# Opening a decoder step with three output tiles instead of two

## The chip, the cores and the metric

The kernel runs on one core of one Trainium2 chip. The metric is device time in microseconds (us) of one execution. In the profile PE is the matrix engine, PEld its weight loads, DVE the vector engine, ACT the scalar engine, POOL the GpSimd engine and SP the engine that only issues transfers (DMAs).

## The reference, cut to what matters

One inference step of a two-layer decoder (one pooling layer, one sliding-window attention layer) for 1024 prompt tokens and 8 single decode tokens, width 2048, all in fp32. The part that concerns us is the first product of the first layer:

```python
def pool_layer(x, prefix, pos, w_in, w_grp, scale, w_out, g_ln, b_ln):
    z = x @ w_in                       # (1032 x 2048) @ (2048 x 4096)
    u, gate = z[..., :D_POOL], z[..., D_POOL:]
    d, new_state = multiscale_pool(u, prefix, pos)
    d = jnp.einsum('btgc,gce->btge', d.reshape(B, T, N_POOL_GROUPS, POOL_GROUP), w_grp)
    ...
    y = (d * jax.nn.silu(gate)) @ w_out
    return layer_norm(ALPHA * x + y, g_ln, b_ln), new_state
```

After it come a shared key/value projection, the attention layer with a second pair of projections, and two layer norms.

## The kernel before, in words

There are four large projections, which the code calls phases: `ai` and `ao` (in and out of the pooling layer), `bi` and `bo` (in and out of the attention layer). Each is a two-by-two block product with seven block products instead of eight (Winograd's form of Strassen's method), numbered by `idx` 0 to 6. The tokens form two parts (512 prompt tokens, and 512 prompt plus 8 decode tokens); depth and output channels form two halves each, in tiles of 128. A **unit** is one block product for one output tile: `pos` is the tile, `idx` the block product, `ph` the phase, and `u.t` is its start in **ticks**, the planner's clock; a unit of group A takes two ticks. Groups are worked in the order A (`idx` 0 and 5), C (1, 3, 6), B (2, 4). `idx` 0 of the phase `ai` reads the even depth tiles of the first token part; `idx` 5 reads the odd ones (the "odd inputs") and adds into the same PSUM bank.

Every fp32 operand is rounded to the fp32r format on ACT (the *high* part, a CAST) and the rest is taken on DVE (the *low* part, high subtracted from the original). A product is then three matmuls with 512 columns: high weight by high input, high by low, low by high. A unit of group A has eight depth blocks, so 24 matmuls.

PSUM gives these products a ring of three banks (`psD`), one bank per output tile. After `idx` 0 ACT copies the bank, negated, to SBUF, which POOL's queue stores to DRAM (`post`, then `nai`); `idx` 5 goes on adding in the same bank, and after it ACT copies the bank out as the result. The bank is then free for a later tile.

The order of the work is written by the program itself. PE, DVE and ACT run strictly in the order in which the Python code records instructions. `end()` closes a tick: it runs tasks fixed to a tick (`on`, e.g. loads 11 ticks ahead of a unit), then "soft" tasks (`soft`: not before one tick, due at another) as far as the engines look idle by rough cost figures. `rounds` queues the two rounding steps of a unit's weights that way; `x_cast`, `x_low` and `x_next` do the same for inputs, and `xhold` keeps the rounding of four odd inputs back until a tick. SBUF is 53 slots of 128 by 1040 fp32, handed out oldest-freed first, halves apart where half is enough.

The start is written out by hand. `start` warms PE with nine matmuls on zeros, then loads the weights of the first two tiles in pieces (a quarter, a quarter, a half of 512 KB) and the four even inputs in halves (260 KB each), all on SP's queue but one on ACT's, and splits each piece into high and low as it comes. The load of the first unit of `idx` 5 and the four odd inputs follow. `opening` then records the matmuls of the first two units: depth blocks 0 to 4 side by side (block 0 of tile 0, block 0 of tile 1, block 1 of tile 0, and so on), blocks 5 to 7 one tile after the other. Inside it, after each tile's last block, the odd inputs' roundings are recorded and the bank is copied. From then on `run_unit` does one unit after the other. Transfers from SP and ACT take turns on eight completion semaphores, and an issue waits for the transfer that last used its semaphore: at most eight are under way.

Of the kernel before, what the change touches and what calls it, by code (L numbers as in the profile page):

```python
# [72 lines left out]
L_LOAD, L_CAST, L_LOW = 11, 6, 4  # L73
# [87 lines left out]
class Kern:  # L161
# [169 lines left out]
    def plan(self):  # L331

        U = self.units = []
        for ph in PH:
            for grp, idxs in GROUPS:
                for pp in range(len(POS[ph]) // 2):
                    two = 2 * pp, 2 * pp + 1
                    U0 = lambda p, i, hs, **kw: U.append(Unit(kind="p", ph=ph, grp=grp, pos=p, idx=i, hs=hs, **kw))
                    if grp == "A":
                        for i in idxs:  # L340
                            if i == 0 and pp in DEEP.get(ph, ()):
                                U.append(Unit(kind="q", ph=ph, grp=grp, pos=two[0], idx=0, hs=(FULL, None) * 2))
                                continue
                            for p in two:
                                U0(p, i, (FULL, None))
                    elif (ph, grp) == ("bo", "B") and pp > 1:
                        continue
                    else:
                        for p in two:
                            for i in idxs:  # L350
                                U0(p, i, HV)
                    if ph == "ai" and pp % 4 == 3:
                        g = pp // 4
                        for c, gg in {"A": ((0, g),), "C": ((0, g + 2),), "B": ((1, g), (1, g + 2))}[grp]:
                            for h in range(2):
                                U.append(Unit(kind="g", ph=ph, grp=grp, c=c, g=gg, h=h, hs=HV))
        for h in HV:
            for p in (4, 6):
                for i in (2, 4):
                    for q in (p, p + 1):  # L360
                        U.append(Unit(kind="p", ph="bo", grp="B", pos=q, idx=i, hs=(h,), keep=h is HV[0]))
        t = 0
        self.first, self.tick, self.need, self.lastu = {}, {}, {}, {}
        for u in U:
            u.t = t
            t += len(u.hs)
# [24 lines left out]
    def rounds(self, t, e, early=L_CAST + 2):  # L391

        def cast():
            if "cast" not in e["did"]:
                e["did"].add("cast")
                if "raw" not in e and "load" in e:
                    e["load"]()
                e["hi"] = self.mem.full()
                self.nc.scalar.copy(e["hi"].r[:, :1024], e["raw"].a[:, :1024])  # L399

        def low():
            if "low" not in e["did"]:
                e["did"].add("low")
                cast()
                s = e.pop("raw")
                o = e["lo"] = self.mem.full()
                self.nc.vector.tensor_sub(o.r[:, :1024], s.a[:, :1024], e["hi"].a[:, :1024])  # L407
                s.free()

        e["did"] = set()  # L410
        e["cast"], e["low"] = cast, low
        def cast_task():
            cast()
            self.soft("v", self.i + 1, t - L_LOW, low)

        e["queue"] = lambda: self.soft("a", max(t - early, 3 * (t > 5)), t - L_CAST + 1, cast_task)
        if "load" in e:
            e["queue"]()

# [302 lines left out]
    def opening(self, *us):  # L722
        nc, cs = self.nc, FULL
        W = [self.w_get(u) for u in us]
        ps = [self.psD() for _ in us]
        for p, u in enumerate(us):
            self.bank[u.ph, u.pos, cs.start] = ps[p]
        todo = [(k, p) for k in range(5) for p in range(2)] + [(k, p) for p in range(2) for k in (5, 6, 7)]

        def three(k, p, zs):  # L730
            h, l = (a.rv(2, TMAX)[:, k % 2, cs] for a in self.x_get(("ai", 0, k // 2)))
            wh, wl = (a.r[:, k * P : (k + 1) * P] for a in W[p])
            for z in zs:
                a, b = ((wh, h), (wh, l), (wl, h))[z]
                nc.tensor.matmul(ps[p], a, b, start=k == 0 and z == 0, stop=k == 7 and z == 2, skip_group_check=True)

        for n, (k, p) in enumerate(todo):
            if n == 0:
                for p in (0, 1):
                    three(0, p, (0,))  # L740
                for p in (0, 1):
                    three(0, p, (1, 2))
            elif n > 1:
                three(k, p, range(3))
            if n == 12:
                self.w_done(us[0])
                self.x_cast(("ai", 5, 0))
                self.x_low(("ai", 5, 0))
                self.post(us[0], cs)
                self.x_cast(("ai", 5, 1))  # L750
                self.x_low(("ai", 5, 1))
            if n == 15:
                self.w_done(us[1])
                self.post(us[1], cs)
                for j in (2, 3):
                    self.x_cast(("ai", 5, j))
            if n % 4 == 3:
                self.end()

# [1432 lines left out]
    def start(self):  # L2192
# [6 lines left out]
        es = [u.ent for u in self.units[:4]]  # L2199
        ks = [self.xl.pop(0) for _ in range(4)]  # L2200
        W, X = ([self.mem.full() for _ in range(n)] for n in (2, 4))
        ws = [slice(256 * i, 256 * i + 256) for i in range(4)]
        xs = [slice(TMAX * i, TMAX * i + TMAX) for i in range(2)]
        src = [self.x_src(k)[1] for k in ks]
        w = [self.quads("ai", p)[0] for p in range(2)]

        def wload(p, c):
            nc.sync.dma_start(W[p].a[:, c], w[p][:, c])

        wload(0, ws[0])  # L2210
        nc.scalar.dma_start(X[0].a[:, xs[0]], src[0][:, 0, :])
        wload(1, ws[0])
        nc.sync.dma_start(X[0].a[:, xs[1]], src[0][:, 1, :])
        for p in range(2):
            wload(p, ws[1])
        for j in range(1, 4):
            for i in range(2):
                nc.sync.dma_start(X[j].a[:, xs[i]], src[j][:, i, :])
            if j == 1:
                for p in range(2):  # L2220
                    wload(p, slice(512, 1024))
        es[2]["load"]()
        for n in range(4):
            self.x_load(self.xl[0])
        es[3]["load"]()
        for j in range(4):
            self.xhold["ai", 5, j] = 3
        nc.sync.dma_start(self.cst[:], io["cst"])
        nc.sync.dma_start(self.prm[:], io["prm"])
        nc.sync.dma_start(self.mki[:], io["mki"])  # L2230
        wn, xn = ([(self.mem.full(), self.mem.full()) for _ in range(n)] for n in (2, 4))

        def split(s, n, c, late=False):
            nc.scalar.copy(n[0].r[:, c], s.a[:, c])
            low = lambda: nc.vector.tensor_sub(n[1].r[:, c], s.a[:, c], n[0].a[:, c])
            return low if late else low()
# [1 line left out]
        low = split(W[0], wn[0], ws[0], True)  # L2238
        split(X[0], xn[0], xs[0])
        low()  # L2240
        split(W[1], wn[1], ws[0])
        split(X[0], xn[0], xs[1])
        for p in range(2):
            split(W[p], wn[p], ws[1])
        for i in range(2):
            split(X[1], xn[1], xs[i])
        for p in range(2):
# [35 lines left out]
    def run(self):  # L2283
# [35 lines left out]
        for g in range(2):  # L2319
            t = f["ai", "B"] + 40 * g  # L2320
# [166 lines left out]
```

## Time and profile before

| | |
|---|---|
| median of 3 runs | 2275.99 us (2271.91 to 2276.68) |
| profiled execution | 2273.81 us |
| its span, first to last instruction | 2272.0 us |
| mean granted PE clock | 0.999 |
| PE busy | 2262.4 us, 17312 matmuls |
| DVE busy | 1598.4 us |
| ACT busy | 1136.1 us |
| memory traffic | 239 GB/s over the span |

The time of a run is some 2 us longer than the span of the profiled execution. Matmuls are pipelined, and the profile gives a matmul's duration from its issue to its modelled end, so "busy" on PE also covers waits that are shorter than a matmul. The pace of PE is therefore read from the start times of its matmuls.

### The profile page before, as it was taken

What the parts mean: (1) busy time and instruction counts of PE and PEld (TensorE: products, weight loads), DVE (VectorE), ACT (ScalarE), POOL (GpSimd) and SP (SyncE); (2) the same over time, 40 slices, a digit from 0 to 9 for tenths busy, and PEclk for the clock granted to TensorE, in tenths of its full rate; (3) what the DMA queues carried; (4) which work ended last, traced back from release to release, by engine and by line L of the source; (5) the groups of instructions that cost most, each with busy time, mean ns of one, the idle gap of its engine ahead of it and who ended that gap; (6) DMA issues with size and microseconds to landing.
All of it is one profiled execution on the core that took longest, in us unless ns stands there. A gap on an engine that the chain in (4) does not pass through costs nothing.

```text
span 2272.0 us, 42903 instructions
## 1 busy us (share of the span) xinstructions
PE 2262.4 (100%) x17312; PEld 2130.5 (94%) x17312; DVE 1598.4 (70%) x2009; ACT 1136.1 (50%) x2372; POOL 197.8 (9%) x418
## 2 busy tenths in 40 slices
PE   9999999999999999999999999999999999999998
PEld 7889999999999899999888899999999998889998
DVE  7667746746667587685786876666566879687688
ACT  6344333343334443454576644545647678553365
POOL 0101001100100111000011010101000000111000
PEclk9999999999999999999999999999999999999999
DMA  9859757673657898888488776666754556898873
GB/s 305 314 209 350 233 213 256 227 249 117 243 184 261 276 336 291 292 304 297 153 295 301 245 244 205 230 195 220 244 169 124 177 189 224 284 356 304 301 250 132
DMA packets 190262, 556.43 MB, mean 245 GB/s; under 512 B 26096, under 2 KB 31600, under 8 KB 190064
## 3 DMA queue, kind: packets, MB, share of 16 engines
q1 hardware_dynamic: 147936, 401.82, 54.0%
q0 software_dynamic: 41984, 151.61, 17.4%
q8 instruction: 135, 2.21, 0.4%
q14 instruction: 63, 0.52, 0.1%
q10 hardware_dynamic: 144, 0.27, 0.0%
HBM read 371.88 MB, written 171.16 MB: 239 GB/s over the span
## 4 chain that ended last, share of the span: by engine, by line
PE 96%; DVE 2%; ACT 1%; DMA 0%; issue 0%; SPq 0%; ACTq 0%; DVEq 0%
PE pD L784 28%; PE pD L786 28%; PE pD L785 28%; PE pD L1351 4%; PE pO L1962 2%; PE pS L1880 2%; PE pS L1933 1%; PE pD L848 1%; DVE m L619 0%; DMA m<-in_wia 0%; DVE m L407 0%; PE pO L848 0%; DMA m<-in_x 0%; PE pO L2087 0%; DVE m L1693 0%
## 5 line engine op out<-in xcount | busy, mean ns | idle before, releaser
L784 PE MATMUL pD<-m,m 128*128 128x260 f32 (+1 forms) x4736 | 1428.6, 302 | 0.4 <-ACT m L894 0.4
L786 PE MATMUL pD<-m,m 128*128 128x260 f32 (+1 forms) x4736 | 1420.7, 300 | 0.0
L785 PE MATMUL pD<-m,m 128*128 128x260 f32 (+1 forms) x4736 | 1420.2, 300 | 0.2 <-DVE m L619 0.2
L784 PEld LDWEIGHTS pD<-m,m 128*128 128x128 f32 x4736 | 891.7, 188 | 38.8 <-issue 5.5
L786 PEld LDWEIGHTS pD<-m,m 128*128 128x128 f32 x4736 | 891.4, 188 | 32.7
L785 PEld LDWEIGHTS pD<-m,m 128*128 128x128 f32 x4736 | 891.8, 188 | 31.9 <-DVE m L619 0.6
L407 DVE TENSOR_TENSOR m<-m,m 128x1024 fp32r<-128x1024 f32 x358 | 435.1, 1218 | 144.2 <-ACT m L399 118.9
L399 ACT CAST m<-m 128x1024 fp32r<-128x1024 f32 x358 | 373.0, 1045 | 48.4 <-DVE m L443 11.7
L443 DVE TENSOR_TENSOR m<-m,m 128x1024 f32<-128x1024 f32 x200 | 243.8, 1219 | 10.4 <-DMA m<-in_woa 2.5
L915 ACT COPY m<-pD 128x260 f32<-128x260 f32 (+1 forms) x126 | 56.0, 444 | 306.4 <-PE pD L786 306.0
L619 DVE TENSOR_TENSOR m<-m,m 128x1040 fp32r<-128x1040 f32 x108 | 130.0, 1234 | 24.1 <-ACT m L613 11.8
L924 ACT ACTIVATE m<-pD 128x260 f32<-128x260 f32 x100 | 38.7, 387 | 180.8 <-PE pD L786 172.7
L926 DVE TENSOR_TENSOR m<-pD,m 128x260 f32<-128x260 f32 x100 | 42.6, 426 | 113.0 <-PE pD L786 109.8
L613 ACT CAST m<-m 128x1040 fp32r<-128x1040 f32 x108 | 111.2, 1061 | 14.6 <-DVE m L407 6.7
L1915 ACT ACTIVATE m<-m,sm 128x128 f32<-128x128 f32 x256 | 99.2, 392 | 0.0
L1351 PE MATMUL pD<-m,m 128*128 128x260 f32 (+1 forms) x576 | 91.5, 319 | 0.0
L1351 PEld LDWEIGHTS pD<-m,m 128*128 128x128 f32 x576 | 82.0, 188 | 8.3
L896 ACT COPY m<-pD 128x260 f32<-128x260 f32 x68 | 25.6, 377 | 124.9 <-PE pD L786 124.9
L1945 DVE TENSOR_TENSOR m<-m,cst 128x1024 f32<-128x1024 f32 x32 | 39.1, 1221 | 69.0 <-ACT m L1941 68.7
L1928 ACT ACTIVATE m<-m,sm 128x128 f32<-128x128 f32 x256 | 81.8, 395 | 7.1 <-DVE sm L1923 7.1
L881 ACT ACTIVATE m<-pD 128x512 f32<-128x512 f32 x50 | 29.8, 597 | 99.4 <-PE pD L786 90.6
L894 ACT ACTIVATE m<-pD 128x260 f32<-128x260 f32 x68 | 26.4, 388 | 101.3 <-PE pD L786 101.3
(246 smaller groups left out, 1857.1 us busy)
## 6 DMA issues: line engine op xcount, KB each, us to landing
m<-in_wib SPq DMA_DIRECT2D x96, 512.0 KB, 5.0
m<-in_wia SPq DMA_DIRECT2D x94, 512.0 KB, 5.6
m<-in_woa SPq DMA_DIRECT2D x48, 512.0 KB, 6.2
m<-in_wob SPq DMA_DIRECT2D x48, 512.0 KB, 7.0
sbi<-m POOLq DMA_DIRECT2D x36, 512.0 KB, 4.2
m<-sbi SPq DMA_DIRECT2D x36, 512.0 KB, 4.5
m<-in_x SPq DMA_DIRECT2D x32, 520.0 KB, 7.4
sai<-m POOLq DMA_DIRECT2D x32, 512.0 KB, 3.9
```

Source lines behind the costliest of these rows:

```text
L399: self.nc.scalar.copy(e["hi"].r[:, :1024], e["raw"].a[:, :1024])
L407: self.nc.vector.tensor_sub(o.r[:, :1024], s.a[:, :1024], e["hi"].a[:, :1024])
L443: self.nc.vector.tensor_add(s[o].a[:, :1024], s[a].a[:, :1024], s[b].a[:, :1024])
L613: self.nc.scalar.copy(h.r[:, : 2 * TMAX], s.a[:, : 2 * TMAX])
L619: self.nc.vector.tensor_sub(o.r[:, : 2 * TMAX], s.a[:, : 2 * TMAX], h.a[:, : 2 * TMAX])
L784: nc.tensor.matmul(ps[:, :w], wh[:, s], h, start=new and n2 == 0, stop=False, skip_group_check=on)
L785: nc.tensor.matmul(ps[:, :w], wh[:, s], l, start=False, stop=False, skip_group_check=on)
L786: nc.tensor.matmul(ps[:, :w], wl[:, s], h, start=False, stop=n2 == 7, skip_group_check=on)
L915: self.evac(ph, pos)(self.dest(ph, pos, m, 0)(cs), ps[:, : cs.stop - cs.start])
L1351: nc.tensor.matmul(ps[:, : cs.stop - cs.start], ws[:, s], d[:, cs], start=f0 and k == 0, stop=l0 and k == 3,)
L1915: nc.scalar.activation(x["s3"][:, i, :], x["s3"][:, i, :], AF.Exp, bias=nm[:, i : i + 1], scale=0.125, accum_out=rs[:, i : i + 1],)
L1928: nc.scalar.activation(x["s3"][:, i, :], x["s3"][:, i, :], AF.Copy, scale=rs[:, i : i + 1])
```

## The change

The first three output tiles are now computed side by side in each of the depth blocks 0 to 4, and one after the other in blocks 5 to 7. The third tile's `idx` 0 is moved ahead of the `idx` 5 units of tiles 0 and 1 (the new first line in `plan`); the units after it keep their order, and the fourth tile's `idx` 0 comes after those two. `start` loads and splits the third tile's weights in the same pieces as the first two. In `opening` the roundings of the odd inputs are spread: each tile's last block is followed by one input's rounding, the copy of that tile's bank, and another's high part. The odd inputs are held until tick 5 instead of 3, and the weights of units later than tick 7 are not rounded before tick 5 (those later than tick 5, not before tick 3, as before). No arithmetic is added or left out.

```diff
+        U[:8] = [U[i] for i in (0, 1, 4, 2, 3, 5, 6, 7)]
...
-        e["queue"] = lambda: self.soft("a", max(t - early, 3 * (t > 5)), t - L_CAST + 1, cast_task)
+        e["queue"] = lambda: self.soft("a", max(t - early, 3 * (t > 5) + 2 * (t > 7)), t - L_CAST + 1, cast_task)
...
-        todo = [(k, p) for k in range(5) for p in range(2)] + [(k, p) for p in range(2) for k in (5, 6, 7)]
+        todo = [(k, p) for k in range(5) for p in range(3)] + [(k, p) for p in range(3) for k in (5, 6, 7)]
...
-            if n == 12:
-                self.w_done(us[0])
-                self.x_cast(("ai", 5, 0))
-                self.x_low(("ai", 5, 0))
-                self.post(us[0], cs)
-                self.x_cast(("ai", 5, 1))
-                self.x_low(("ai", 5, 1))
-            if n == 15:
-                self.w_done(us[1])
-                self.post(us[1], cs)
-                for j in (2, 3):
-                    self.x_cast(("ai", 5, j))
+            if n in (17, 20, 23):
+                self.w_done(us[p])
+                if p < 2:
+                    self.x_cast(("ai", 5, p))
+                    self.x_low(("ai", 5, p))
+                self.post(us[p], cs)
+                if p:
+                    self.x_cast(("ai", 5, p + 1))
...
-        W, X = ([self.mem.full() for _ in range(n)] for n in (2, 4))
+        W, X = ([self.mem.full() for _ in range(n)] for n in (3, 4))
...
         wload(1, ws[0])
+        wload(2, ws[0])
         nc.sync.dma_start(X[0].a[:, xs[1]], src[0][:, 1, :])
-        for p in range(2):
+        for p in range(3):
             wload(p, ws[1])
...
-        es[2]["load"]()
+        es[3]["load"]()
...
-            self.xhold["ai", 5, j] = 3
+            self.xhold["ai", 5, j] = 5
...
-        self.opening(*self.units[:2])
-        for u in self.units[2:]:
+        self.opening(*self.units[:3])
+        for u in self.units[3:]:
```

**SP's queue from the first load.** Before, `m_2` and `m_3` are the raw weights of the two tiles and `m_4` to `m_7` the four raw even inputs; the text in brackets is the semaphore that the issue waits for.

```order
L2208 DMA m_2_173<-in_wia 128x256
L2208 DMA m_3_174<-in_wia 128x256
L2213 DMA m_4_175<-in_x 128x520
L2208 DMA m_2_173<-in_wia 128x256
L2208 DMA m_3_174<-in_wia 128x256
L2218 DMA m_5_176<-in_x 128x520 x2
L2208 DMA m_2_173<-in_wia 128x512 [waits DMAHW0_49]
L2208 DMA m_3_174<-in_wia 128x512 [waits DMAHW1_49]
L2218 DMA m_6_177<-in_x 128x520 [waits DMAHW2_49]
```

Now `m_2`, `m_3` and `m_4` are the weights of three tiles and `m_5` to `m_8` the inputs:

```order
L2205 DMA m_2_173<-in_wia 128x256
L2205 DMA m_3_174<-in_wia 128x256
L2205 DMA m_4_175<-in_wia 128x256
L2211 DMA m_5_176<-in_x 128x520
L2205 DMA m_2_173<-in_wia 128x256
L2205 DMA m_3_174<-in_wia 128x256
L2205 DMA m_4_175<-in_wia 128x256
L2216 DMA m_6_177<-in_x 128x520 [waits DMAHW0_49]
L2216 DMA m_6_177<-in_x 128x520 [waits DMAHW1_49]
L2205 DMA m_2_173<-in_wia 128x512 [waits DMAHW2_49]
```

The two halves of the second even input (`m_5` before, `m_6` now) were issued without a wait; now two more quarters of weights stand ahead of them and the first half waits for semaphore 0, which is that of the transfer on ACT's queue (the first half of the first input).

**PE from the first real matmul.** Before, `pD_252` and `pD_253` are the banks of tiles 0 and 1, `m_18` and `m_19` high and low of the first input, `m_14` and `m_15`, `m_16` and `m_17` high and low of the two tiles' weights:

```order
L735 MATMUL pD_252<-m_18_212,m_14_208 128x512
L735 MATMUL pD_253<-m_18_212,m_16_210 128x512
L735 MATMUL pD_252<-m_19_213,m_14_208 128x512
L735 MATMUL pD_252<-m_18_212,m_15_209 128x512
L735 MATMUL pD_253<-m_19_213,m_16_210 128x512
L735 MATMUL pD_253<-m_18_212,m_17_211 128x512
L735 MATMUL pD_252<-m_18_212,m_14_208 128x512
```

Now with `pD_262` to `pD_264`, input `m_21` and `m_22`, weights `m_15` to `m_20`:

```order
L736 MATMUL pD_262<-m_21_218,m_15_212 128x512
L736 MATMUL pD_263<-m_21_218,m_17_214 128x512
L736 MATMUL pD_264<-m_21_218,m_19_216 128x512
L736 MATMUL pD_262<-m_22_219,m_15_212 128x512
L736 MATMUL pD_262<-m_21_218,m_16_213 128x512
L736 MATMUL pD_263<-m_22_219,m_17_214 128x512
L736 MATMUL pD_263<-m_21_218,m_18_215 128x512
L736 MATMUL pD_264<-m_22_219,m_19_216 128x512
L736 MATMUL pD_264<-m_21_218,m_20_217 128x512
L736 MATMUL pD_262<-m_21_218,m_15_212 128x512
```

A depth block is nine matmuls instead of six, and the opening 72 instead of 48.

**DVE behind the last even input.** Before, L407 is the low part of the weights of the first `idx` 5 unit, L649 a sum of raw even inputs for a later product, and the L619 rows are the low parts of the four odd inputs:

```order
L2235 TENSOR_TENSOR m_25_219<-m_7_178,m_24_218 128x520 x2
L407 TENSOR_TENSOR m_30_282<-m_8_193,m_28_266 128x1024
L649 TENSOR_TENSOR m_31_296<-m_4_175 128x512
L619 TENSOR_TENSOR m_36_306<-m_9_195,m_35_304 128x1040
L619 TENSOR_TENSOR m_39_314<-m_10_197,m_38_312 128x1040
L619 TENSOR_TENSOR m_45_337<-m_11_199,m_41_329 128x1040
L619 TENSOR_TENSOR m_46_339<-m_12_201,m_42_331 128x1040
```

Now the same work is L408, L650 and L620:

```order
L650 TENSOR_TENSOR m_31_303<-m_5_176 128x512
L650 TENSOR_TENSOR m_33_305<-m_7_178,m_5_176 128x512
L650 TENSOR_TENSOR m_32_304<-m_7_178,m_31_303 128x512
L650 TENSOR_TENSOR m_34_306<-m_7_178,m_32_304 128x512
L650 TENSOR_TENSOR m_31_303<-m_6_177 128x512
L620 TENSOR_TENSOR m_38_336<-m_10_199,m_37_334 128x1040
L408 TENSOR_TENSOR m_40_348<-m_9_197,m_36_322 128x1024
L620 TENSOR_TENSOR m_42_355<-m_11_201,m_41_353 128x1040
```

Five sums instead of one now stand ahead of the first odd input's low part, and the first `idx` 5 unit's weights come behind it.

More of the change, by code (lines that the diff above doesn't have):

```diff
@@ L738, in opening @@
             if n == 0:
-                for p in (0, 1):
+                for p in (0, 1, 2):
                     three(0, p, (0,))
-                for p in (0, 1):
+                for p in (0, 1, 2):
                     three(0, p, (1, 2))
-            elif n > 1:
+            elif n > 2:
                 three(k, p, range(3))
-            if n == 12:
-                self.w_done(us[0])
-                self.x_cast(("ai", 5, 0))
-                self.x_low(("ai", 5, 0))
-                self.post(us[0], cs)
-                self.x_cast(("ai", 5, 1))
-                self.x_low(("ai", 5, 1))
-            if n == 15:
-                self.w_done(us[1])
-                self.post(us[1], cs)
-                for j in (2, 3):
-                    self.x_cast(("ai", 5, j))
+            if n in (17, 20, 23):
[6 more added lines that the diff above has]
+                    self.x_cast(("ai", 5, p + 1))
             if n % 4 == 3:
@@ L2198, in start @@
             nc.tensor.matmul(ps[:, :144], z.a[:, :P], z.a[:, :144], start=True, stop=True)
-        es = [u.ent for u in self.units[:4]]
+        es = [u.ent for u in self.units[:5]]
         ks = [self.xl.pop(0) for _ in range(4)]
-        W, X = ([self.mem.full() for _ in range(n)] for n in (2, 4))
+        W, X = ([self.mem.full() for _ in range(n)] for n in (3, 4))
         ws = [slice(256 * i, 256 * i + 256) for i in range(4)]
@@ L2204, in start @@
         src = [self.x_src(k)[1] for k in ks]
-        w = [self.quads("ai", p)[0] for p in range(2)]
+        w = [self.quads("ai", p)[0] for p in range(3)]
         def wload(p, c):
@@ L2219, in start @@
             if j == 1:
-                for p in range(2):
+                for p in range(3):
                     wload(p, slice(512, 1024))
-        es[2]["load"]()
+        es[3]["load"]()
         for n in range(4):
             self.x_load(self.xl[0])
-        es[3]["load"]()
+        es[4]["load"]()
         for j in range(4):
-            self.xhold["ai", 5, j] = 3
+            self.xhold["ai", 5, j] = 5
         nc.sync.dma_start(self.cst[:], io["cst"])
@@ L2230, in start @@
         nc.sync.dma_start(self.mki[:], io["mki"])
-        wn, xn = ([(self.mem.full(), self.mem.full()) for _ in range(n)] for n in (2, 4))
+        wn, xn = ([(self.mem.full(), self.mem.full()) for _ in range(n)] for n in (3, 4))
         def split(s, n, c, late=False):
@@ L2240, in start @@
         low()
-        split(W[1], wn[1], ws[0])
+        for p in (1, 2):
+            split(W[p], wn[p], ws[0])
         split(X[0], xn[0], xs[1])
-        for p in range(2):
+        for p in range(3):
             split(W[p], wn[p], ws[1])
@@ L2246, in start @@
             split(X[1], xn[1], xs[i])
-        for p in range(2):
+        for p in range(3):
             split(W[p], wn[p], slice(512, 1024))
```

## The prediction

> **What bounds the kernel now.** First the page's busy times and its chain of work, then the busy time of each engine by stretch, then the opening row by row.
>
> ```profile
> PE 2262.4 (100%) x17312; PEld 2130.5 (94%) x17312; DVE 1598.4 (70%) x2009; ACT 1136.1 (50%) x2372; POOL 197.8 (9%) x418
> PE 96%; DVE 2%; ACT 1%; DMA 0%; issue 0%; SPq 0%; ACTq 0%; DVEq 0%
> 0.00:5.64 5.64, 3.91 (x18) 3.70 (x18) 0.02 (x1) 2.26 (x4) 0.82 (x10) 1.00 0.65 206
> 5.64:18.98 13.34, 12.90 (x51) 9.44 (x52) 11.48 (x18) 10.79 (x18) 0.83 (x2) 1.00 0.99 361
> 18.98:42.00 23.02, 23.02 (x101) 18.64 (x100) 19.08 (x25) 15.79 (x22) 1.43 (x5) 1.00 0.95 344
> 42.00:2266.00 2224.00, 2222.57 (x17145) 2098.75 (x17143) 1565.86 (x1962) 1105.44 (x2328) 194.75 (x401) 1.00 0.72 243
> 2266.00:2272.00 6.00, 0.00 (x0) 0.00 (x0) 2.01 (x6) 1.78 (x4) 0.00 (x0) 0.87 0.67 227
> ```
>
> In the stretches the first two numbers are length and PE's busy time, the last three are granted clock, DMA share and GB/s. PE is the bound from 5.64 us to 2266: after 42 us it is idle for 2224.00 - 2222.57 = 1.43 us in all, and the last 6.00 us are stores behind it. A change in the opening can give only what PE loses between its first real matmul (5.64) and the steady run (18.98), plus what it breaks later.
>
> ```profile
> 96.37 11.14 PE pD L1351 x48
> 5.64 6.50 PE L735 MATMUL pD<-m,m 128*128 128x512 f32 x25 [0.72 <-ACT m L2234]
> 12.38 5.60 PE L735 MATMUL pD<-m,m 128*128 128x512 f32 x23 [0.23 <-DVE m L2235]
> 17.81 0.40 PE L784 MATMUL pD<-m,m 128*128 128x512 f32 x1
> 18.41 0.50 PE L785 MATMUL pD<-m,m 128*128 128x512 f32 x1 [0.20 <-DVE m L619]
> 18.98 0.40 PE L784 MATMUL pD<-m,m 128*128 128x512 f32 x1
> 5.64:7.27 1.63, 1.63 (x5) 1.00 1.06 297
> ```
>
> The first row, from the chain, gives the pace: 11.14 / 48 = 0.232 us for a matmul of 512 columns. From 5.64 to 18.98 PE starts 25 + 23 + 3 = 51 matmuls: 51 x 0.232 = 11.83, so 13.34 - 11.83 = 1.51 us are lost. They lie in three places. The first five take 1.63 instead of 1.16, loss 0.47. The next twenty, to 12.38, take 5.11 instead of 4.64, loss 0.47: the low part of the third even input was late (DVE L2235). The last three, from 17.81, take 1.17 instead of 0.70, loss 0.47: the low part of the first odd input was late (DVE L619). The remaining 0.1 is spread.
>
> **The change part by part.** PE does the same matmuls; only the order and the loads differ. I compare the moment at which PE starts its 73rd matmul, since 72 are the new opening. Before, that is 18.98 + 21 x 0.232 = 23.85.
>
> *Start.* The first matmul needs the first quarter of weights and the first half of input 0, which are still the first transfer on SP and the one on ACT:
>
> ```profile
> 0.74 0.89 SPq L2208 DMA_DIRECT2D m<-in_wia  x2
> 3.10 0.92 SPq L2218 DMA_DIRECT2D m<-in_x  x2
> 4.47 0.80 SPq L2208 DMA_DIRECT2D m<-in_wia  x2
> 4.66 2.38 ACT L2234 CAST m<-m 128x256 fp32r<-128x256 f32 x6 [2.21 <-DMA m<-in_wia]
> 7.27 1.32 ACT L2234 CAST m<-m 128x520 fp32r<-128x520 f32 x2 [0.24 <-DMA m<-in_x]
> 9.68 3.94 ACT L2234 CAST m<-m 128x512 fp32r<-128x512 f32 x6 [1.08 <-DMA m<-in_wia]
> 14.29 1.05 ACT L399 CAST m<-m 128x1024 fp32r<-128x1024 f32 x1 [0.67 <-DMA m<-in_wia]
> 15.64 1.06 ACT L613 CAST m<-m 128x1040 fp32r<-128x1040 f32 x1 [0.30 <-DMA m<-in_x]
> L2234 ACT CAST m<-m 128x520 fp32r<-128x520 f32 x8 | 5.0, 626 | 0.5 <-DMA m<-in_x 0.2
> L2235 DVE TENSOR_TENSOR m<-m,m 128x520 fp32r<-128x520 f32 x8 | 5.4, 697 | 5.6 <-ACT m L2234 5.6
> L2235 DVE TENSOR_TENSOR m<-m,m 128x256 fp32r<-128x256 f32 x4 | 1.5, 417 | 0.0
> 14.00:18.00 4.00, 4.00 (x19) 3.06 (x17) 2.98 (x4) 3.41 (x4) 0.28 (x2) 1.00 1.05 394
> ```
>
> So it stays at 5.64. Block 0 gets a third matmul that needs a high part alone, which fills a step in which PE waited for DVE, but one cast and one low part (417 ns) more stand in the queues. Bounds for the loss 0.28 (one step of 0.23 filled, less rounding) and 0.47 + 0.31 = 0.78 (one more step of ACT in series); I keep 0.47, since DVE, which ends last there, still delivers a tile's low part in 0.42 us against three matmuls (0.70).
>
> *Second input, first half.* Its issue goes from 3.10 to about 4.47, the moment at which the ninth transfer in all, SP's eighth, got its semaphore. This is the place where the change can lose. In the rows above it landed at 7.27 (ACT waited for it), 4.17 us after its issue; the transfer issued at 4.47, a half of the first weights, landed at 9.68, 5.21 us after. So the bounds are 4.47 + 4.17 = 8.64 and 9.68. Ahead of the 9.68 transfer were 4 x 128 + 4 x 260 = 1552 KB; ahead of this one are now 6 x 128 + 2 x 260 = 1288 KB, 264 KB less, at 394 GB/s 0.69 us. I take 9.68 - 0.69 = 8.99. PE wants the high part at 5.64 + 0.47 + 18 x 0.232 = 10.29 and the low part at 10.52. It gets the low part at 8.99 + 0.63 + 0.70 = 10.32: no wait. At the late bound it comes at 11.01, a loss of 0.49, 0.6 with a slow restart.
>
> [...]
>
> *Third and fourth input.* Between that half and the fourth input's last half now stand 260 + 768 + 1040 = 2068 KB, 5.37 us at 394 GB/s: 14.36, late bound 15.05. With 0.63 + 0.70 its low part is there by 15.69 to 16.38; tile 0 wants it at 5.64 + 0.47 + 52 x 0.232 = 18.17. The third input's first half comes after 1288 KB, 3.35 us: low part at 13.67 to 14.36, wanted at 5.64 + 0.47 + 37 x 0.232 = 14.69. So the loss of 0.47 at 12.38 goes. What hides these loads is twelve matmuls more (2.8 us) per four blocks; without them the 512 KB, 1.33 us, would lie on the path.
>
> *Odd inputs.* The opening ends at 5.64 + 0.47 + 72 x 0.232 = 22.81. The weights of the first `idx` 5 unit and the first odd input landed at 14.29 and 15.64, 1.35 apart; behind the fourth input they now land at about 15.7 to 16.4 and 17.1 to 17.8.
>
> ```profile
> 16.61 0.59 ACT L881 ACTIVATE m<-pD 128x512 f32<-128x512 f32 x1
> 15.38 1.23 DVE L407 TENSOR_TENSOR m<-m,m 128x1024 fp32r<-128x1024 f32 x1 [1.02 <-ACT m L399]
> 16.52 0.68 DVE L649 TENSOR_TENSOR m<-m 128x512 f32<-128x512 f32 x1
> 19.63 2.43 DVE L619 TENSOR_TENSOR m<-m,m 128x1040 fp32r<-128x1040 f32 x2
> ```
>
> On DVE five sums of 0.68 run from 16.4 to 19.8, then low parts of 1.23: first odd input at 21.0, weights 22.3, second 23.5, third 24.7, fourth 26.0. On ACT the casts of 1.06 stand behind the copies of the banks, which wait for PE at 18.64, 20.73 and 22.81, plus 0.59 each: 20.6, 22.6 and 24.7 for inputs two to four, ahead of DVE each time. PE wants the low parts at 23.0, 23.3, 24.4, 25.8, 27.2. All are there with at least 0.9 us to spare, so the third loss of 0.47 goes too.
>
> *Later.* ACT gets 0.4 us more of casts and DVE 0.3 more of low parts (weights in three pieces); both have 30% idle and more. POOL's queue gets the third bank's store earlier. The third tile's own 512 KB load leaves SP's later queue, so later loads lose no place. The next weights were cast at 24.09 and wanted at 18.98 + 45 x 0.232 = 29.42:
>
> ```profile
> 24.09 1.05 ACT L399 CAST m<-m 128x1024 fp32r<-128x1024 f32 x1 [2.05 <-DMA m<-in_wia]
> 25.17 1.23 DVE L407 TENSOR_TENSOR m<-m,m 128x1024 fp32r<-128x1024 f32 x1 [1.87 <-ACT m L399]
> ```
>
> They were ready at 26.40, 3.0 us early. Now the fourth tile's come first, wanted at 22.81 + 48 x 0.232 = 33.95, and even 1.8 us later they are 5.7 us early. After some 50 us PE, DVE and ACT run in the same order as before, and on SP only neighbours trade places. I cost the rest at nothing.
>
> *Sum.* 23.85 - 22.81 = 1.04 us gained, between 0.4 (second input late) and 1.2 (start at its best). The profiled execution would go from 2273.81 to about 2272.8. It lies 2.18 below the median of the runs, so for the median I say 2275.99 - 1.0 = 2275.0. That is 0.05%, and 0.2% (4.55 us) is about what a measurement of this kernel can tell from no change, the three runs alone spreading over 4.77 us.
>
> **The rivals.** *A: the second input eats the gain.* Issue to landing of the inputs, with a full queue, took up to 6.2 us:
>
> ```profile
> DMA to landing us min/median/max: 4.2/5.7/6.2
> ```
>
> Then the half lands at 10.67, its low part comes at 12.0, PE waits 1.5 us, and the change ends 0.4 to 0.6 us slower. Against it: the queue is emptier than for those. It decides from a landing after about 10.2.
>
> *B: slower by over 0.2%.* Weights for the units right after the opening come late, since the DMA engines are 0.95 busy from 18.98 to 42 and the eight-semaphore order holds SP up. By the spare time above the fourth tile's weights would have to come 5.7 + 1.04 + 4.55 = 11.3 us later than I reckon; ACT's 2.05 idle before 24.09 shows that loads are what ends last there. Against it: the bytes are the same and PE wants them later. It would give 2280.6 or more.
>
> *C: clock.* PE is granted half its clock once, for 3.4 us:
>
> ```profile
> 1939.30:1942.70 3.40, 3.40 (x10) 2.69 (x9) 1.62 (x4) 0.21 (x1) 0.00 (x0) 0.51 0.94 365
> ```
>
> Half of 3.4, 1.7 us, is its price. If the shift of 1 us makes it fall away, the gain is 2.7 and the time 2273.3; one more dip gives 2275.99 - 1.04 + 1.7 = 2276.7. The Trainium skill's page "TensorE: Matmul & The Clock Gate", Part 1, has free-running windows of about 3.4 us whose activity sets the clock, which fits the length of this row; by it a dip can come or go with a shift, but the opening's waits of under 1 us, at clock 1.00 in the rows above, should not bring one.
>
> *Faster by over 0.2%* has no mechanism: all that PE loses from 5.64 to 18.98 is 1.51 us, and 1.43 after 42.
>
> **How the numbers follow.** Forecast (gain of 0.4 to 1.2) 0.72, A 0.10, C 0.12 for both sides together, B 0.06. All but B lie within 0.2%; since the runs scatter and the forecast is on the fast side, I move 0.07 of it to faster: faster 0.07, same 0.87, slower 0.06. The range is set by the runs more than by the terms: the fastest run less the full gain, 2271.91 - 1.2 = 2270.7, and the slowest with A and half a dip, 2276.68 + 0.6 + 0.9 = 2278.2.
>
> **What would show it.** In the new profile the opening's matmuls should be 72 from about 5.64, the first `idx` 5 matmul should start near 22.8 with no idle before it, and no PE wait on DVE should stand between 8 and 34 us. A wait of PE near 10.3 us for ACT or DVE, with ACT waiting for an input just before, is A. A wait near 34 us is B. I am wrong if PE loses microseconds after 42 us, where I count on the order being unchanged.

## The result, and the profile after

The changed kernel takes 2279.72 us (median; 2277.79 to 2283.09) against 2274.30 for the kernel before in the same runs. The ratio is 1.0022, 95% interval 1.0015 to 1.0029: slower by about 5 us, where 1 us less was forecast. The profiled execution has a span of 2277.0 us, before 2272.0. First the page's span, busy times and chain of work, then the stretches cut as in the prediction.

```profile
span 2277.0 us, 42924 instructions
PE 2264.0 (99%) x17312; PEld 2132.3 (94%) x17312; DVE 1599.5 (70%) x2011; ACT 1136.2 (50%) x2374; POOL 197.5 (9%) x418
PE 95%; DVE 2%; DMA 1%; ACT 1%; issue 0%; SPq 0%; DVEq 0%; ACTq 0%
```

```profile
0.00:5.32 5.32, 4.31 (x18) 4.32 (x18) 0.02 (x1) 2.26 (x4) 0.81 (x10) 1.00 0.63 184
5.32:18.98 13.66, 13.59 (x59) 10.59 (x59) 12.02 (x22) 10.13 (x18) 0.11 (x1) 1.00 1.01 360
18.98:42.00 23.02, 23.02 (x101) 18.64 (x100) 20.15 (x23) 17.80 (x24) 2.80 (x8) 1.00 0.96 356
42.00:2271.00 2229.00, 2223.11 (x17140) 2098.79 (x17138) 1565.48 (x1964) 1104.41 (x2327) 193.79 (x399) 1.00 0.71 243
2271.00:2277.00 6.00, 0.00 (x0) 0.00 (x0) 1.82 (x5) 1.57 (x4) 0.00 (x0) 0.87 0.65 222
```

By 18.98 PE has started 59 real matmuls (third number of the second row), before 51: the opening is better. The loss is in the long row. PE is idle there for 2229.00 - 2223.11 = 5.89 us, before 1.43. The waits of PE, by what ended them (us in all, times, longest):

```profile
PE pS L1877 <- ACT m L1938: 3.3, 1, 3.3
PE pO L2195 <- POOL m L877: 1.0, 1, 1.0
PE pS L1877 <- DVE m L1860: 0.9, 1, 0.9
PE pO L1804 <- ACT m L921: 0.5, 1, 0.5
```

The second and the fourth stand before too. The first and the third are new, both in the attention layer, long after the opening. Comparing the start of every PE matmul with the same matmul of before gives the ledger: the lead is 1.19 us at the end of the opening (22.65 against 23.84) and stays between 0.8 and 1.35 to 1220 us; 0.3 is lost at 1224, 1.1 at 1278.6, 3.4 at 1909.55, and 1.5 in the few us behind that, of which 0.3 come back by 1927. -1.2 + 0.3 + 1.1 + 3.4 + 1.5 - 0.3 = +4.8 for a span that grew by 5.0.

**The wait at 1909 us.** L614 (L613 before) is a high part of an input of the phase `bo`. From the timelines of before:

```profile
1896.32 0.73 POOL L1050 DMA_DIRECT2D to<-m  x1
1898.78 2.03 ACT L613 CAST m<-m 128x1040 fp32r<-128x1040 f32 x2
1902.81 2.07 SPq L603 DMA_DIRECT2D m<-o  x3
1903.33 1.00 ACT L1941 COPY m<-pS 128x1024 f32<-128x1024 f32 x1
```

And from those of the changed kernel:

```profile
1896.35 0.73 POOL L1047 DMA_DIRECT2D to<-m  x1
1898.84 1.06 ACT L614 CAST m<-m 128x1040 fp32r<-128x1040 f32 x1
1904.93 1.06 ACT L614 CAST m<-m 128x1040 fp32r<-128x1040 f32 x1 [5.03 <-DVE m L923]
1908.50 0.99 ACT L1938 COPY m<-pS 128x1024 f32<-128x1024 f32 x1
1909.55 2.45 PE L1877 MATMUL pS<-m,m 64*128 64x256 f32 x24 [3.27 <-ACT m L1938]
```

The view of that POOL store alone, from issue to landing:

```profile
DMA to landing us min/median/max: 8.5/8.5/8.5
```

Before, two casts ran back to back (x2). After, the second stands 5.03 us; everything behind it on ACT moves by that, among it the copy of line 1938, which frees what PE needs. The row names a DVE instruction as the releaser (L923, done at 1904.54), but the value of DVE's semaphore that the cast waits for is the one that the store of POOL itself waited for (1636 in the program), and so it was reached before 1896.35. The cast starts 0.1 us after 1896.35 + 8.5 = 1904.85, when that store lands. What the cast has to do with that store stands in the program's own slot names (slot, then number of the allocation) and waits. Of the kernel before, ACT, SP and POOL:

```
L613 CAST m18_1957_21122<-m2_1931_20756 128x1040 [waits DMAHW2_49]
L603 DMA m25_1958_21124<-o0_144 128x2x520 [waits DMAHW6_49,DMAHW4_49,DMASW5_49]
L1050 DMA to_143<-m25_1934_20829 128x2x512 [waits DMAHW6_49,DMASW5_49,DVE_49]
```

and of the changed kernel:

```
L614 CAST m15_1957_21128<-m1_1931_20762 128x1040 [waits DMAHW0_49,DMAHW4_49,DMASW5_49,DVE_49]
L604 DMA m21_1958_21130<-o0_144 128x2x520 [waits DMAHW5_49,PE_49]
L1047 DMA to_143<-m15_1934_20835 128x2x512 [waits DMAHW0_49,DMASW5_49,DVE_49]
```

The order of the instructions is the same. But tile 1957, the cast's destination, now lies in the slot of tile 1934, which is still being stored, and has taken over the wait on that store (DMASW5); tile 1958, an input load on SP, has got the idle slot. Before it was the other way round: SP waited there instead (its load into slot 25 is issued at 1903.99, 0.02 us behind the store's landing), and no wait of PE came of it.

Why they traded: `full` takes the slot with the lowest release number, where a release counts one and a stored tile is given 10 on top. At allocation 1957 two slots have the same number, 1945: the one of tile 1698, released then, and the one of tile 1934, released at 1935 and stored. `min` takes the lower slot number. Before, 1698 lay in slot 18 and 1934 in slot 25; after, 1934 lies in slot 15 and 1698 in slot 21. The opening with three tiles allocates in another order and so renumbers the slots; from allocation 330 on 38 pairs of neighbouring allocations trade their slots, this one and 1354/1355 and 1366/1367 among them.

**The clock behind it.** Two stretches of the changed kernel have half the clock (the third number from the end: 0.54 and 0.51 granted):

```profile
1909.90:1913.40 3.50, 3.50 (x28) 2.99 (x25) 2.63 (x5) 3.45 (x10) 0.10 (x1) 0.54 0.97 381
1944.30:1947.80 3.50, 3.50 (x10) 2.67 (x8) 1.33 (x3) 0.00 (x0) 0.00 (x0) 0.51 1.03 390
```

The second is the dip that the kernel before has at 1939. The first follows on the pause and costs the 1.5.

**The waits at 1224 and 1278 us.** At 1278 the input for the VectorE sum L443 (L444 after) came late, and the sum held up L1860 behind it on DVE, for which PE waits. The semaphore that the sum waits for is that of the load of `in_wkv` issued at 1265.82 before and at 1264.73 after. Before, with an earlier load, then after, with the same earlier load and the next one (x2):

```profile
1257.88 0.33 SPq L435 DMA_DIRECT2D m<-in_wkv  x1
1265.82 0.51 SPq L435 DMA_DIRECT2D m<-in_wkv  x1
1274.31 1.22 DVE L443 TENSOR_TENSOR m<-m,m 128x1024 f32<-128x1024 f32 x1 [1.66 <-DMA m<-in_wkv]
```

```profile
1260.82 1.02 SPq L436 DMA_DIRECT2D m<-in_wkv  x2
1264.73 1.36 SPq L436 DMA_DIRECT2D m<-in_wkv  x1
1275.58 1.23 DVE L444 TENSOR_TENSOR m<-m,m 128x1024 f32<-128x1024 f32 x1 [3.29 <-DMA m<-in_wkv]
1278.61 1.45 PE L1877 MATMUL pS<-m,m 64*128 64x256 f32 x20 [0.91 <-DVE m L1860]
```

The load that the sum needs is issued 1.09 us earlier than before and lands 1.26 us later: at 1275.48 against 1274.22, which is 10.7 us after its issue against 8.4. Ahead of it, the load that went out at 1257.88 now goes out at 1260.82, behind four transfers from slot to slot (`m<-m`) and only 0.6 us ahead of the next one. The tie of 1366 and 1367 decides this, as the runs below show. That two loads close together make the third one land late is read from these rows and those runs and was not tried by itself; nor is it worked out how the tie reorders the loads.

### The profile page after: what moved, and what is told of

It is laid out like the page before. It is cut to its first block, busy times and chain, and to the rows that moved or that the text cites. A ratio compares the mean times of both kernels' runs of the same rounds, so it can differ in the third digit from the quotient of the medians.

```text
span 2277.0 us, 42924 instructions
## 1 busy us (share of the span) xinstructions
PE 2264.0 (99%) x17312; PEld 2132.3 (94%) x17312; DVE 1599.5 (70%) x2011; ACT 1136.2 (50%) x2374; POOL 197.5 (9%) x418
## 4 chain that ended last, share of the span: by engine, by line
PE 95%; DVE 2%; DMA 1%; ACT 1%; issue 0%; SPq 0%; DVEq 0%; ACTq 0%
PE pD L781 28%; PE pD L783 28%; PE pD L782 28%; PE pD L1348 4%; PE pO L1959 2%; PE pS L1877 2%; PE pD L845 1%; PE pS L1930 1%; DMA m<-in_wkv 0%; PE pD L736 0%; DMA m<-m 0%; DMA m<-in_x 0%; ACT m L1912 0%; PE pO L845 0%; DMA m<-in_wia 0%
## 5 line engine op out<-in xcount | busy, mean ns | idle before, releaser
L408 DVE TENSOR_TENSOR m<-m,m 128x1024 fp32r<-128x1024 f32 x357 | 434.0, 1219 | 143.3 <-ACT m L400 119.6
L444 DVE TENSOR_TENSOR m<-m,m 128x1024 f32<-128x1024 f32 x200 | 244.0, 1220 | 12.8 <-DMA m<-in_woa 3.9
L620 DVE TENSOR_TENSOR m<-m,m 128x1040 fp32r<-128x1040 f32 x108 | 130.0, 1235 | 25.2 <-ACT m L614 11.2
L614 ACT CAST m<-m 128x1040 fp32r<-128x1040 f32 x108 | 111.3, 1061 | 30.1 <-DMA tg<-m 10.8
L923 DVE TENSOR_TENSOR m<-pD,m 128x260 f32<-128x260 f32 x100 | 42.6, 426 | 113.0 <-PE pD L783 109.7
L878 ACT ACTIVATE m<-pD 128x512 f32<-128x512 f32 x50 | 29.8, 597 | 93.4 <-PE pD L783 71.9
```

What stands on the lines that cost most here:

```text
L444: self.nc.vector.tensor_add(s[o].a[:, :1024], s[a].a[:, :1024], s[b].a[:, :1024])
L614: self.nc.scalar.copy(h.r[:, : 2 * TMAX], s.a[:, : 2 * TMAX])
L620: self.nc.vector.tensor_sub(o.r[:, : 2 * TMAX], s.a[:, : 2 * TMAX], h.a[:, : 2 * TMAX])
```

## The experiments

The theory from here on (theory 1 in the expectations): the opening does what it should, and every loss behind it is a tie in the slot pool that now falls the other way. Its rivals: the loss comes from arriving earlier at a place where transfers collide (theory 2), from the clock alone, or from the delayed casts. A tie is turned round for chosen allocations by taking the second of the sorted slots:

```diff
     def full(self):
-        i = min(self.whole(), key=lambda i: max(self.f[i]))
+        c = sorted(self.whole(), key=lambda i: max(self.f[i]))
+        i = c[1] if self.n + 1 in (1957,) else c[0]
```

### The changed kernel with tie 1957 turned round

The edit is the diff above, on the changed kernel.

> The changed kernel, with one choice among equally old slots of the SBUF pool turned round: allocation 1957 (the destination of a ScalarE cast) and allocation 1958 (an input load) trade their slots, so that the cast no longer gets the slot whose store to memory is still in flight. Theory 1 (the tie is the cause of the stall at 1909 us): the 3.3 us wait of the fourth-stage matmuls on the ScalarE copy of line 1938 goes, and the half-clock window of 3.4 us behind it with it, so that the span falls by 3.4 to 4.9 us to 2272.1 to 2273.6, and the ratio to the kernel before is 0.9990 to 1.0010. Theory 2 (the stall comes from an earlier arrival at 1909 us or from the load on the DMA queues): the stall stays, 2276 to 2278, ratio 1.002. Theory 3 (clock alone): the pause goes but a half-clock window stays, 2273.5, ratio 1.0007.

Measured: ratio 1.0000 (0.9991 to 1.0009), span 2272.9. The two casts run back to back again in ACT's timeline:

```profile
1899.81 2.02 ACT L615 CAST m<-m 128x1040 fp32r<-128x1040 f32 x2
```

and the stretch has no pause and full clock:

```profile
1904.00:1916.00 12.00, 12.00 (x94) 9.66 (x93) 11.86 (x17) 9.42 (x23) 0.33 (x2) 1.00 0.83 267
```

One choice of a slot, with the opening, the casts and the order untouched, brings back the difference between 1.0022 and 1.0000, some 5 us, while 1.3 us at 1278 stay. The ratios tell this better than the two spans, since this execution has no dip near 1940 and leads by only 0.6 us after the opening. Theory 2 and the clock alone fall for this part.

### The kernel before with the same tie turned round

The same diff on the kernel before.

> The kernel before, opening untouched, with the same two allocations 1957 and 1958 trading slots; every other slot has the tenants that it had. Theory 1: a wait of some 3 us on the ScalarE copy of line 1938 appears near 1909 us, 3.3 to 4.9 us in all with a half-clock window behind it, ratio 1.0014 to 1.0022. Theory 2: no wait, ratio 1.0000 within 0.0005.

Measured: ratio 1.0019 (1.0011 to 1.0028), span 2276.7. The stall appears in a kernel with the old opening, in PE's waits:

```profile
PE pS L1881 <- ACT m L1942: 3.4, 1, 3.4
```

in ACT's timeline:

```profile
1905.52 1.06 ACT L614 CAST m<-m 128x1040 fp32r<-128x1040 f32 x1 [5.07 <-DVE m L927]
```

and in the stretch behind it, with a granted clock of 0.51:

```profile
1909.50:1916.50 7.00, 6.36 (x33) 5.41 (x34) 5.02 (x7) 6.46 (x17) 0.10 (x1) 0.51 0.93 348
```

That stretch is twice as long here as in the changed kernel (7 us); the dip near 1940 is absent from this execution. So the tie is both enough to make the stall and, by the run above, needed for it. Of the thirteen profiles told here the five in which 1957 gets the slot of 1934 have the stall, and none of the other eight.

### The changed kernel with the slots of before

85 ties turned round, so that from allocation 330 on each tile lies where the same earlier tile lay before (but for 2314 and 2315, three from the end).

```diff
+        i = c[1] if self.n + 1 in (332, 354, 359,
...
+            1354, 1366, 1410,
...
+            1957, 2017, 2042,
...
+            2314) else c[0]
```

> The changed kernel, with 85 choices among equally old slots turned round, so that from allocation 330 on each tile lies where the same earlier tile lay as in the kernel before. Theory 1: all three losses (0.3 us at 1224, 0.7 at 1278, 3.4 and the half-clock window at 1909) go, and the opening's gain of 1.2 us stays to the end: span 2270.5 to 2271.2, ratio 0.9990 to 0.9997, faster than both kernels. Theory 2: 2276 to 2278, ratio 1.002.

Measured: ratio 0.9995 (0.9986 to 1.0003), span 2270.0. No PE wait at 1278 or 1909. PE is 1.28 us ahead at the end of the opening; 0.3 us are lost at 1224 here too, against theory 1, and 0.9 us of the lead are left at 1905. Run once more:

> The lineage kernel once more, for its ratio: with the opening's gain of 1.2 us and none of the three losses 0.9993 to 0.9997 of the kernel before; no wait over 0.3 us at 1225, 1278 or 1909 us.

Measured: ratio 0.9996 (0.9987 to 1.0004), span 2272.6, again without those waits and without the loss at 1224, 1.47 us ahead at the end of the opening and 1.4 at 1905. Both values are what such leads make of 2274 (0.9996 and 0.9994); each interval still reaches to just over 1, so that the times alone don't prove a gain, while the traces show the lead. It is the best kernel of this study. The second of these two executions of one kernel (on two chips) is 0.5 us ahead until 1937, and yet its span is 2.6 us longer: it loses 3.1 us in the stretch 1937 to 1945. The rows are of the first run and of the second:

```profile
1937.00:1945.00 8.00, 8.00 (x57) 6.61 (x57) 5.36 (x9) 3.98 (x11) 0.10 (x1) 1.00 0.85 310
```

```profile
1937.00:1945.00 8.00, 8.00 (x42) 6.33 (x41) 2.58 (x6) 1.07 (x3) 0.10 (x1) 0.59 0.71 264
```

57 matmuls at clock 1.00 against 42 at 0.59. So the dip near 1940 comes and goes between executions of one kernel; seven of the thirteen profiles have it.

### One part of the change undone: the later queueing

```diff
-        ... max(t - early, 3 * (t > 5) + 2 * (t > 7)) ...
+        ... max(t - early, 3 * (t > 5)) ...
```

> The changed kernel with one part undone: the later queueing of casts (the term with t above 7) is taken out again, the three-tile opening and the longer hold stay. In the slot table allocation 1957 still gets the slot whose store is in flight. Theory 1: the 3.3 us wait near 1909 us stays, ratio 1.0015 to 1.0026. Rival (the delayed casts cause the loss): the wait goes, ratio 0.999 to 1.000.

Measured: ratio 1.0058 (1.0046 to 1.0071), far outside both expectations. The stall at 1909 is there as theory 1 wants it, and so is 0.8 us at 1278. PE's wait for it:

```profile
PE pS L1877 <- ACT m L1938: 2.6, 1, 2.6
```

But 9 us are lost in the opening, which neither foresaw. The timeline of ACT and PE:

```profile
23.71 1.05 ACT L400 CAST m<-m 128x1024 fp32r<-128x1024 f32 x1 [5.64 <-DMA m<-in_wia]
27.84 0.59 ACT L878 ACTIVATE m<-pD 128x512 f32<-128x512 f32 x1
28.48 0.79 PE L781 MATMUL pD<-m,m 128*128 128x512 f32 x1 [4.18 <-ACT m L878]
```

and the stretch behind it:

```profile
28.48:34.90 6.42, 6.08 (x12) 3.86 (x13) 6.42 (x7) 5.67 (x7) 1.94 (x4) 0.51 0.93 186
```

Without the later queueing a cast of later weights stands on ACT ahead of the first bank's copy (L878) and waits 5.64 us for its load; the copy, in order behind it, comes at 27.84 instead of 18.75 and PE waits for it, then runs 6.4 us at half clock. So with three tiles the later queueing is needed, and since the stall at 1909 stands without it, it is not the cause of that loss.

### The later queueing alone

The kernel before, two tiles, with only that line changed.

> One part of the change alone: the kernel before, two output tiles in the opening, with the later queueing of casts (the term with t above 7). Its slot table flips 1354 and 1366 but not 1957. Theory 1: no gain in the opening (within 0.4 us of before by 50 us), the 0.7 to 1.3 us at 1278 appear, no stall at 1909; ratio 1.0002 to 1.0010. Rival (the later queueing itself makes casts late after the opening): losses between 25 and 60 us, ratio above 1.001.

Measured: ratio 1.0008 (1.0000 to 1.0017). No gain in the opening and no loss from 25 to 60 us; 1.3 us at 1278 as the flipped tie of 1366 predicts; no stall at 1909. A further 1.1 us at 2027 was not expected: it stands in five of the runs told here (0.8 to 1.2 us) and once differs between two executions of one kernel, and its cause stays open.

### Ties 1354 and 1366 turned round

On the changed kernel the tuple of the first diff is (1354, 1366), 1957 as the change has it:

> The changed kernel with two other ties turned round: allocations 1354 and 1355, and 1366 and 1367, trade their slots, 1957 and 1958 stay as the change has them. Theory 1 (every loss behind the opening is such a tie): the loss of 0.7 to 1.3 us at 1225 to 1278 us (a wait of some 0.9 us on the VectorE add of line 1860) goes, the stall at 1909 us stays at 3 to 3.5 us; ratio to the kernel before 1.0010 to 1.0020. Theory 2 (the loss at 1278 is the changed moment of arrival): the wait at 1278 stays, ratio 1.002.

Measured: ratio 1.0018 (1.0009 to 1.0027), the stall at 1909 is there as it should; but 1.0 us at 1278 stayed, against theory 1. The two earlier loads were again 3.2 us apart, as in the kernel before (3.3), and yet the load that the sum needs, issued at 1264.84, landed late, at 1275.08, 10.2 us after its issue. The run was made again for this (its expectation counts from the issue of the load behind, at 1267.68, which lands only after the sum has run; so its 7.5 and 5.7 us are too short):

> The changed kernel with 1354 and 1366 turned round, once more for its profile: if the 1.0 us at 1278 us that it kept is a load that landed late by chance (7.5 us from issue to landing instead of 5.7), it is gone now; if something else of the slot table makes it, it stands again at 0.8 to 1.2 us. The stall at 1909 us stands in either case.

Measured: this time no wait at 1278, the stall at 1909 again (3.0 us). The load was issued at 1264.79 and landed at 1272.92, after 8.1 us. The VectorE sum behind the load in the first and in the second execution:

```profile
1275.17 1.23 DVE L445 TENSOR_TENSOR m<-m,m 128x1024 f32<-128x1024 f32 x1 [2.94 <-DMA m<-in_wkv]
```

```profile
1273.02 1.23 DVE L445 TENSOR_TENSOR m<-m,m 128x1024 f32<-128x1024 f32 x1 [0.91 <-DMA m<-in_wkv]
```

So the landing alone moves by some 2 us there between two executions of one kernel (on two chips). The same pairs turned round in the kernel before:

> The kernel before with the same two pairs (1354 and 1355, 1366 and 1367) turned round. Theory 1: a wait of 0.7 to 1.3 us on the VectorE add of line 1860 appears at 1278 us and nothing else, ratio 1.0003 to 1.0007. Theory 2: no wait, ratio 1.0000.

Measured: 0.9 us at 1278 (a PE wait of 0.8 on L1864), nothing else new; ratio 1.0004 (0.9995 to 1.0013). And the kernel with the slots of before, but these two pairs as the change deals them:

> The kernel of the lineage run (slots re-dealt as in the kernel before) with the two pairs 1354 and 1355, 1366 and 1367 left as the change deals them. Theory 1: the wait on the VectorE add of line 1860 is back at 1278 us with 0.7 to 1.3 us and no stall at 1909; against the lineage run of the same chip +0.8 us, ratio 1.0000 against 0.9996. Rival (at 1278 us the load's landing varies by itself, since the DMA engines are full there): no wait, or one in the lineage run too.

Measured: ratio 1.0001 (0.9992 to 1.0010) against 0.9996 of its twin, and the wait is back:

```profile
1278.79 1.46 PE L1878 MATMUL pS<-m,m 64*128 64x256 f32 x20 [1.07 <-DVE m L1861]
```

The wait at 1278 stands in all seven profiles in which the pair 1366 is dealt as the change deals it, and in one of the six with the dealing of before. In the seven the two earlier loads are 0.6 to 1.3 us apart and the load that the sum needs lands 9.6 to 11.1 us after its issue. In the six they are 3.2 to 3.8 us apart and it lands after 8.1 to 8.6 us, or 10.2 in the one with the wait. The run without the later queueing deals 1366 as the change does and 1354 as before, so that of the two pairs 1366 is enough. So the tie makes this loss, about 1 us, but a late landing can make it too. The 0.3 us at 1224 I can't assign: the kernel before with only 1957 turned round lost 0.5 there, and the first run with the slots of before 0.3.

### A rule in place of hand-picked ties

The changed kernel, with a note `hot` for each slot on whether its last tile was stored. Among slots with the same release number one whose last tile was not stored is taken first.

```diff
-        i = min(self.whole(), key=lambda i: max(self.f[i]))
+        i = min(self.whole(), key=lambda i: (max(self.f[i]), self.hot[i]))
...
+            self.hot[s.i] = late
```

> The changed kernel with a rule in place of the hand-picked swaps: among equally old slots the pool takes one whose last tile was not stored to memory first. By its slot table 1957 gets the slot without a store again, 1354 and 1366 stay flipped. Theory 1: no stall at 1909, the 0.7 to 1.3 us at 1278 stay, opening gain 0.6 to 1.2 us: ratio 0.9996 to 1.0004. Theory 2: 1.002.

Measured: ratio 1.0008 (0.9999 to 1.0017), outside the expectation, though far better than the change. The stall at 1909 is gone, 1.6 us stand at 1278, and a rule turns other ties as well: 2.3 us are lost at 1171 and 1192, among them

```profile
1192.25 1.21 PE L1932 MATMUL pS<-cst,m 128*128 128x128 f32 x4 [0.95 <-ACT m L1927]
```

That these come from ties that the rule turned was not tried one by one. Preferring the slot without a store is right for 1957, but no rule on the tie alone says which of the two takers can afford to wait.

## Why the prediction was right and wrong

*Bound.* PE, and the opening could give up to 1.51 us: held.

*Start.* Predicted to stay at 5.64 with a first block's loss of 0.47. It came at 5.32. Rows of the changed kernel's ACT, SP and PE in the opening:

```profile
4.34 1.57 ACT L2232 CAST m<-m 128x256 fp32r<-128x256 f32 x4 [1.89 <-DMA m<-in_wia]
4.15 0.80 SPq L2216 DMA_DIRECT2D m<-in_x  x2
8.47 0.63 ACT L2232 CAST m<-m 128x520 fp32r<-128x520 f32 x1 [0.69 <-DMA m<-in_x]
16.40 1.05 ACT L400 CAST m<-m 128x1024 fp32r<-128x1024 f32 x1 [0.79 <-DMA m<-in_wia]
17.78 1.07 ACT L614 CAST m<-m 128x1040 fp32r<-128x1040 f32 x1 [0.32 <-DMA m<-in_x]
5.32 17.48 PE L736 MATMUL pD<-m,m 128*128 128x512 f32 x72
22.65 0.40 PE L781 MATMUL pD<-m,m 128*128 128x512 f32 x1
```

The first quarter of weights landed 0.3 us earlier than before (ACT's cast at 4.34, then 4.66). The three-tile kernels' profiles start between 5.13 and 5.46, the two-tile ones between 5.43 and 5.76, so most of it goes with the change; why the first transfer lands earlier is open. From 5.32 the 72 matmuls would end at 5.32 + 72 x 0.232 = 22.02; they end at 22.65, so the opening still loses 0.63, against the 0.47 kept in the sum.

*Second input.* Issue 4.15 (4.47 predicted), landing 8.47 (8.99, bounds 8.64 to 9.68): 4.32 us, inside the two durations used (4.17 and 5.21). No wait of PE for it; rival A is out.

*Third input, odd inputs.* Weights of the first `idx` 5 unit at 16.40 (15.7 to 16.4 predicted), first odd input at 17.78 (17.1 to 17.8), first `idx` 5 matmul at 22.65 (22.81), with no idle time ahead of it. Both losses went, and no PE wait stands on DVE between 8 and 34 us. Rival B, late weights right after the opening, is out. The gain at the 73rd matmul is 1.19 for 1.04. That the two are so close is in part luck: 0.32 of it is the earlier start, which was not forecast, and 0.16 went to the larger loss inside the opening. The gain itself is no accident of one execution: over the eight profiles with three tiles and the later queueing the 73rd matmul starts at 22.38 to 23.26, over the four with two tiles at 23.72 to 24.16.

*Later.* This is the step that failed: "After some 50 us PE, DVE and ACT run in the same order as before, and on SP only neighbours trade places. I cost the rest at nothing." The sentence on the order was true of PE, DVE and ACT, though on SP some loads move further (the one issued at 1257.88 goes behind four transfers), and the conclusion was not true. The order is what the program writes; what an instruction waits for is also set by which tile had its slot before, and the change renumbers the slots. The term that I set to 0 was 0.3 + 1.1 + 3.4 + 1.5 - 0.3 = 6.0 us. The runs assign all of it but the 0.3 at 1224 to two ties: the stall and the half clock behind it to 1957, the 1.1 at 1278 to 1366. The loads that trade places on SP were its visible end. The last sentence of the prediction named the place (microseconds after 42 us), and no rival had a mechanism for it; with a slot table of both kernels side by side, 1957 would have shown as a cast that took over a store's wait.

*Clock.* Rival C allowed for one more dip at 1.7 us; one came, at 1.5, but as the follower of a pause and not by a shift. The dip near 1940 stands in both profiles (1939 before, 1944 after) and so makes no difference between them.

## What to carry to other kernels

When a change alters the order of early allocations, compare not only the order of instructions but, tile by tile, whose slot each one takes over: a flipped tie far behind the edit can put an in-order engine behind a store in flight (here 5 us of ACT, 3.4 of PE, and a half-clock window on top). Before a change of 1 us is judged, give the kernel the old hand-out of slots; then the change and the reshuffle can be told apart, here 0.9995 and 1.0022. A slot whose last tile is still being stored belongs to a taker that nobody waits for, such as a load far ahead.

## What the runs showed of the hardware

Six PE pauses of 3.0 to 4.6 us (from one matmul's start to the next) stand in these profiles, and each was followed by a stretch of half clock: 3.4 us long in the changed kernel, 7 in the kernel before with 1957 turned round, 6.4 in the opening without later queueing, where also a gap of 1.6 us at 11 us was followed by clock 1.00. The Trainium skill's page "TensorE: Matmul & The Clock Gate", Part 1, puts the return to half speed at an idle window of about 3.4 us. Five of the pauses (3.4 to 4.6 us) agree; the one of 3.0 us is shorter and brought half clock as well, so that here a little less was enough. Pauses don't explain the dip near 1940, which comes and goes between executions of one kernel at a place where PE is busy in the profile (2.00 of 2.00 us from 1937 to 1939 before); what stands there are 27 matmuls with only 16 columns in 3.17 us, and whether these count as idle was not tried. The scatter goes with the clock: of the 21 executions of the kernel before beside the last runs, the six with a mean clock of 1.0 have a median span of 2271.1, the ten with 0.999 of 2272.7, the five with 0.998 of 2275.1. That the dips make this difference fits their price but is not shown, since only profiled executions show dips.

A 512 KB store took 8.5 us from issue to landing at 1896, and a 512 KB load issued at 1264.8 took 8.1 us in one execution and 10.2 in another of the same kernel, with the DMA engines at full share (1.02 and 1.04 from 1264.8 to 1275).
